# Prompt attention taken in pairs: one TensorE visit for two items, softmax statistics stored in runs, the samples' decoding queued at a group's last value slab

## The chip, the core and the metric

The kernel runs on one core of a Trainium2 chip. The metric is device time in microseconds (us), the median of three runs. The profile is of one further execution. TensorE is called PE in the rows (its weight loads PEld), VectorE is DVE, ScalarE is ACT, GpSimd is POOL, and SP is the queue from which nearly all DMAs are issued.

## What is computed

One layer of a decoder trunk for 1024 prompt tokens and 8 samples of 4 tokens, width 1024. Cut to what matters here:

```
h, B, C, q, k, v, g_conv, g_att = xn @ w_in          # q, k, v: 3 groups x 8 heads x 64
conv_out = (B * causal_conv3(C * h)) @ w_conv_out
for g, (window, dil) in enumerate(((128, 1), (512, 4), (2048, 16))):
    logits = q . k[t - i * dil] * scale + bias[i]    # i = 0 .. window / dil
    m = max(logits); p = exp(logits - m); s = sum(p); o_g = p @ v / s
o = merge of the three groups by their softmax denominators
x = x + gate1 * ((sig(g_conv) * conv_out + sig(g_att) * (o @ w_attn_out)) @ w_o)
x = x + gate2 * (relu(norm(x) @ w_mlp_in) ** 2 @ w_mlp_out)
```

The samples' tokens attend to caches of earlier keys and values (the decoding).

## The kernel before

All float32 products are made of three matmuls on split operands (high and low parts). The stages follow each other: gate and convolution projections, then q, k and v, then `w_conv_out`, `w_attn_out`, `w_o`, and the channel mixer.

**The stage of the change.** For each group in `ORDER` = (1, 2, 0) and each of its four pairs of heads (a *unit*), three slabs are projected: q, k and v. Each slab is three `gemm` calls of 24 matmuls (L375, 352 columns). `gemm` calls `slot()` after its 12th matmul and the main loop calls it again after the 24th, so a slot lies behind every 12 matmuls, 18 in a unit. After the last v chunk `add_unit` queues the unit's eight attention *items* (128 queries each, against one or two blocks of 128 keys, `nk`), and they are worked off inside the next unit's slots. After the last unit they run inside the stage of `w_conv_out`, which has 24 `gemm` calls and 48 slots.

**slot()** first runs what `later` holds as due, then lets the generator `attention` (in `bg`) advance while its credit lasts, then the two lanes of `paced` (the decoding and the merges), each of which says how many slots it rests. The credit grows by `rate` per slot: 0.85 of the queued `work` over 18 slots, 2200 after the last unit.

**One item** goes through three steps, pipelined over three items. `att_scores`: six matmuls of 64 rows (L974) into one `ps_s` and one `ps_g` bank, two adds of the bias with a maximum (L976, DVE), the negated maximum (L979), two exponentials (L982, ACT). `att_tr`: 2 x nk transposes by TensorE (L102) and a copy back. `att_pv`: 4 x nk matmuls of 64 columns (L1011) into `ps_o`. Between these steps the credit may run out, and then 12 projection matmuls come in between. Of the 96 items 44 have nk = 2.

**After a unit's last item** `att_pv` writes the maxima and sums (`st`) to `st_d` in DRAM, element by element: a unit's 128 x 32 numbers go as 4096 pieces of 4 bytes, in four DMAs (eight in group 2). `merge(j)` (L1222) reads them back and weights the three groups. PSUM banks: three of `ps_g` (the projections use them too), two of `ps_s`, one each of `ps_pt`, `ps_ss`, `ps_o`. `ps_ss` holds the sums of squares of q and k (L378, L379), read by a chain on ACT (L387 to L389) and DVE (L393).

**The decoding** `decode(g)` starts when the last item of the group's fourth unit is done; that of the last group runs after all attention, one step per slot. It uses `ps_s` and `ps_pt`.

Of the kernel before, what the change touches and what calls it, by code (L numbers as in the profile page):

```python
# [17 lines left out]
P = 128  # L18
# [21 lines left out]
NPG, NHF = 34, 5  # L40
# [9 lines left out]
class Trunk:  # L50
# [53 lines left out]
    def slot(self):  # L104
# [6 lines left out]
        while self.bg and self.credit > 0:  # L111
            try:
                cost = next(self.bg[0])
                if cost is None:
                    break
                self.credit -= cost
            except StopIteration:
                self.bg.popleft()
# [770 lines left out]
    def add_unit(self, g, j, q, k, v):  # L889
        u = dict(g=g, j=j, q=q, k=k, v=v, bias=self.bias, vt=None, O=None, st=None)  # L890
        tiles = self.attn_tiles(g)
        for i, tl in enumerate(tiles):
            self.items.append((u, tl, i == 0, i == len(tiles) - 1, i))
            self.work += 650 + 570 * tl[2]
        self.work += 600

    def values(self, u):
        nc, v = self.nc, u["v"]
        u["vt"] = vt = self.page("vt", (P, 8, P))
        for h in range(2):  # L900
            b = self.bank("s")
# [3 lines left out]
            del b  # L905
            yield None

    def sample_values(self, u):
        g, j = u["g"], u["j"]
        b = self.bank("pt")  # L910
        self.turn(b[0:32, 0:P], u["v"][:, NP:T], self.ident)
        self.evac(self.vnew[32 * g:32 * g + 32, j * P:(j + 1) * P], b[0:32, 0:P])

    def attention(self):
        st = {}
        s1 = s2 = last = None
        while True:
            it = self.items.popleft() if self.items else None
            if last is not None:
                self.sample_values(last)  # L920
                if last["g"] == ORDER[2]:
                    if last["j"] < 3:
                        self.paced[1].append(self.merge(last["j"]))
                elif last["j"] == 3:
                    self.paced[0].append(self.decode(last["g"]))
                last = None
                yield 100.0
            if it is None and s1 is None and s2 is None:
# [4 lines left out]
            if it is not None:  # L933
                if it[2]:
                    if it[0]["bias"] is None:
                        it[0]["bias"] = self.load_bias(it[0]["g"], it[0]["j"])
                    yield from self.values(it[0])
                self.att_scores(it, st)
                yield 650.0
            else:  # L940
                yield None
            if s1 is not None:
                self.att_tr(s1, st)
                yield 220.0 * s1[1][2]
            else:
                yield None
            if s2 is not None:
                self.att_pv(s2, st)
                yield 350.0 * s2[1][2]
                if s2[3]:  # L950
                    last = s2[0]
            s1, s2 = it, s1
        self.paced[1].append(self.merge(3))
        for g in (self.decode(ORDER[2]), self.sample_merge()):
            for n in g:
                for _ in range(n):
                    yield None

    def att_scores(self, it, st):
        nc = self.nc  # L960
        u, tl = it[0], it[1]
        q, k, bias = u["q"], u["k"], u["bias"]
        q0, k0, nk, b0, _, _ = tl
        N = nk * P
        ps = [self.bank(n) for n in "sg"]
        S = self.half("S")
        if u["st"] is None:
            u["st"] = self.sm.tile([P, 2, 2, 8], F32, name="st", tag="st", bufs=3)
        mx, sm = (u["st"][:, x, :, it[4]] for x in range(2))
        ng = self.sm.tile([P, 2], F32, name="ng", tag="ng", bufs=3)  # L970
        for x, (a, b) in enumerate((("hi", "hi"), ("hi", "lo"), ("lo", "hi"))):
            for hh in range(2):
                pr = slice(64 * hh, 64 * hh + 64)
                nc.tensor.matmul(ps[hh][:, :N], q[a][pr, q0:q0 + P], k[b][pr, k0:k0 + N], start=(x == 0), stop=(x == 2))  # L974
        for hh in range(2):
            nc.vector.tensor_tensor_reduce(  # L976
                out=S[:, hh * 256:hh * 256 + N], in0=ps[hh][:, :N], in1=bias[:, hh, b0:b0 + N],
                scale=1.0, scalar=LOW, op0=ALU.add, op1=ALU.max, accum_out=mx[:, hh:hh + 1])
        nc.vector.tensor_scalar(ng, mx, -1.0, None, op0=ALU.mult)  # L979
        for hh in range(2):  # L980
            s = S[:, hh * 256:hh * 256 + N]
            nc.scalar.activation(s, s, AF.Exp, bias=ng[:, hh:hh + 1], accum_out=sm[:, hh:hh + 1])  # L982
        st[id(it)] = S

    def att_tr(self, it, st):
        nk = it[1][2]
        S = st[id(it)]
        ps = self.bank("g" if it[4] % 2 else "pt")
# [7 lines left out]
    def att_pv(self, it, st):  # L996
# [27 lines left out]
        if last:  # L1024
# [3 lines left out]
            for x in range(2):  # L1028
                for hh in range(2):
                    row = sd[x, hh]  # L1030
                    if g == 0:
                        nc.sync.dma_start(out=row.rearrange("(t i) -> i t", i=P), in_=stt[:, x, hh])
                    elif g == 1:
                        nc.sync.dma_start(out=row.rearrange("(q i r) -> i r q", q=2, r=4),
                                          in_=stt[:, x, hh].rearrange("p (r q) -> p r q", q=2))
                    else:
                        for y in range(2):
                            nc.sync.dma_start(out=row.rearrange("(a t y) -> y a t", t=8, y=2)[y],
# [905 lines left out]
```

## Time and profile before

| | |
|---|---|
| time, median of 3 runs | 2187.48 us (2186.69 to 2188.03) |
| the profiled execution | 2182.63 us, of which the span is 2180.8 us |
| busy in the span | PE 2055.5 us (94%), DVE 1416.5 (65%), ACT 995.9 (46%), POOL 785.4 (36%) |
| mean granted clock of TensorE | 0.981 |

The span runs from the first to the last instruction. A share of the whole span is an average over stages. The rows further down are of the stages around the change.

### The profile page before, as it was taken

The page shows a single profiled execution, that of the slowest core. Times are in us where ns is not written, and L with a number is a line of the kernel's source. Part 1 is how long each engine was busy: PE and PEld are TensorE (multiplying, and loading weights), DVE is VectorE, ACT ScalarE, POOL GpSimd, SP SyncE. Part 2 cuts the span into 40 slices and gives each one's busy share as a digit, 9 for nine tenths or more (in the row PEclk, how much of TensorE's full clock was granted, in tenths as well). Part 3 has the DMA queues.
Part 4 walks back from the last instruction along what each step waited for, and adds up shares of the span by engine and source line. Part 5 has one row for each costly group of instructions (what it writes and reads, how often), then busy time and mean ns, then how long its engine had stood idle before and what let it go on. Part 6 is the DMA issues. An engine that isn't in the chain of part 4 may idle for free.

```text
span 2180.8 us, 38933 instructions
## 1 busy us (share of the span) xinstructions
PE 2055.5 (94%) x15092; PEld 1906.9 (87%) x15092; DVE 1416.5 (65%) x2973; ACT 995.9 (46%) x2195; POOL 785.4 (36%) x553
## 2 busy tenths in 40 slices
PE   5899999999999999999998799998999999999998
PEld 2799999889888888778877689998999998999998
DVE  4846666435555566566666488369444447999997
ACT  4522323335555655455545232346555557433332
POOL 3645565320111110100112113235333335788785
PEclk8999999999999999999998899999999999999999
DMA  7242221664144577766567894541337629556542
GB/s 282 74 131 64 75 73 41 231 215 148 46 59 53 58 150 138 147 122 113 125 166 105 183 313 152 186 137 68 141 148 290 249 85 338 208 186 215 204 152 106
DMA packets 180978, 325.85 MB, mean 149 GB/s; under 512 B 77113, under 2 KB 120761, under 8 KB 179769
## 3 DMA queue, kind: packets, MB, share of 16 engines
q1 hardware_dynamic: 180360, 323.17, 51.9%
q8 instruction: 118, 1.93, 0.5%
q14 instruction: 68, 0.55, 0.1%
q10 hardware_dynamic: 432, 0.20, 0.0%
HBM read 270.48 MB, written 112.07 MB: 175 GB/s over the span
## 4 chain that ended last, share of the span: by engine, by line
PE 52%; DVE 18%; DMA 5%; ACT 4%; issue 3%; SPq 1%; POOL 1%; another core or an unknown queue 0%; DVEq 0%; ACTq 0%; POOLq 0%
PE ps_g L375 23%; DVE acc L1707 5%; DVE wprod L160 4%; PE ps_g L262 3%; PE ps_s L262 3%; PE ps_s L263 3%; PE ps_g L264 3%; PE ps_s L264 3%; PE ps_g L263 3%; PE ps_o L1011 1%; DVE hl L1559 1%; PE ps_s L974 1%; DVE wlo L195 1%; DMA st_d<-st 1%; DMA sg<-gate_d 1%
## 5 line engine op out<-in xcount | busy, mean ns | idle before, releaser
L160 DVE TENSOR_TENSOR wprod<-wraw,wprod 128x512 fp32r<-128x512 f32 x276 | 269.9, 980 | 177.1 <-ACT wprod L156 176.9
L375 PE MATMUL ps_g<-xh,whi 128*128 128x352 f32 x1056 | 367.3, 348 | 12.5 <-ACT whi L191 5.1
L375 PE MATMUL ps_g<-xh,wlo 128*128 128x352 f32 x1056 | 346.3, 328 | 4.2 <-DVE wlo L195 4.1
L375 PE MATMUL ps_g<-xl,whi 128*128 128x352 f32 x1056 | 347.0, 329 | 3.0 <-POOL xl L404 2.1
L375 PEld LDWEIGHTS ps_g<-xh,whi 128*128 128x128 f32 x1056 | 203.1, 192 | 49.5 <-issue 25.5
L156 ACT CAST wprod<-wraw 128x512 fp32r<-128x512 f32 x276 | 163.3, 618 | 151.8 <-DVE wprod L160 104.6
L375 PEld LDWEIGHTS ps_g<-xl,whi 128*128 128x128 f32 x1056 | 203.1, 192 | 6.3 <-POOL xl L404 4.1
L375 PEld LDWEIGHTS ps_g<-xh,wlo 128*128 128x128 f32 x1056 | 202.7, 192 | 5.7 <-DVE wlo L195 5.7
L195 DVE TENSOR_TENSOR wlo<-wraw,whi 128x512 fp32r<-128x512 f32 x184 | 132.1, 760 | 47.6 <-PE ps_g L375 22.3
L160 POOL TENSOR_TENSOR lo<-qn,hi 128x1024 fp32r<-128x1024 f32 x12 | 34.0, 2833 | 358.0 <-ACT hi L156 332.9
L275 POOL TENSOR_TENSOR ps_z<-ps_z,ps_s 128x264 f32<-128x264 f32 x64 | 60.4, 946 | 252.7 <-DVE ps_s L274 252.0
L262 PE MATMUL ps_s<-th,wprod 128*128 128x264 f32 x512 | 145.7, 285 | 1.8 <-DVE ps_s L274 1.8
L262 PE MATMUL ps_g<-th,wprod 128*128 128x264 f32 x512 | 146.8, 287 | 0.0
L263 PE MATMUL ps_s<-tl,wprod 128*128 128x264 f32 x512 | 145.9, 285 | 0.0
L264 PE MATMUL ps_g<-th,wprod 128*128 128x264 f32 x512 | 145.8, 285 | 0.0
L263 PE MATMUL ps_g<-tl,wprod 128*128 128x264 f32 x512 | 145.5, 284 | 0.0
L264 PE MATMUL ps_s<-th,wprod 128*128 128x264 f32 x512 | 145.4, 284 | 0.0
L191 ACT CAST whi<-wraw 128x512 fp32r<-128x512 f32 x184 | 104.5, 619 | 54.8 <-DMA wraw<-in_w_conv_out 40.3
L982 ACT ACTIVATE S<-S,ng 128x128 f32<-128x128 f32 (+1 forms) x192 | 84.9, 443 | 93.1 <-DVE ng L979 91.4
L262 PE MATMUL ps_g<-xh,wprod 128*128 128x264 f32 x384 | 110.7, 288 | 4.6 <-ACT wprod L156 4.6
L262 PE MATMUL ps_s<-xh,wprod 128*128 128x264 f32 x384 | 110.5, 288 | 3.4 <-DVE ps_s L278 3.4
L264 PE MATMUL ps_g<-xh,wprod 128*128 128x264 f32 x384 | 110.3, 287 | 3.5 <-DVE wprod L160 3.5
(386 smaller groups left out, 6617.1 us busy)
## 6 DMA issues: line engine op xcount, KB each, us to landing
wraw<-in_w_in SPq DMA_DIRECT2D x76, 512.0 KB
wada<-in_w_ada SPq DMA_DIRECT2D x48, 512.0 KB
hid_d<-hid SPq DMA_DIRECT2D x32, 528.0 KB
wraw<-in_w_mlp_in SPq DMA_DIRECT2D x32, 512.0 KB
wraw<-in_w_mlp_out SPq DMA_DIRECT2D x32, 512.0 KB
hraw<-hid_d SPq DMA_DIRECT2D x56, 264.0 KB
kv<-in_v SPq DMA_DIRECT2D x28, 512.0 KB
wraw<-in_w_conv_out SPq DMA_DIRECT2D x24, 512.0 KB
```

What stands on the lines that cost most here:

```text
L156: nc.scalar.copy(hi, src)
L160: eng.tensor_tensor(out=lo, in0=src, in1=hi.bitcast(F32), op=ALU.subtract)
L191: self.nc.scalar.copy(hi[:, s], w[:, s])
L195: self.nc.vector.tensor_tensor(out=lo[:, s], in0=w[:, s], in1=hi[:, s].bitcast(F32), op=ALU.subtract)
L262: nc.tensor.matmul(ps, hi, xh, start=(k == 0), stop=False)
L263: nc.tensor.matmul(ps, hi, xl, start=False, stop=False)
L264: nc.tensor.matmul(ps, lo, xh, start=False, stop=(k == 3))
L275: nc.gpsimd.tensor_tensor(out=z[p], in0=z[p], in1=s[p], op=ALU.add)
L375: self.nc.tensor.matmul(ps, a, x, start=(i == 0), stop=(i == n - 1))
L974: nc.tensor.matmul(ps[hh][:, :N], q[a][pr, q0:q0 + P], k[b][pr, k0:k0 + N], start=(x == 0), stop=(x == 2))
L982: nc.scalar.activation(s, s, AF.Exp, bias=ng[:, hh:hh + 1], accum_out=sm[:, hh:hh + 1])
L1707: nc.vector.tensor_tensor(out=a, in0=a, in1=ps, op=ALU.add)
```

## The change

Items leave the queue two at a time. A *visit* is now one uninterrupted piece of work: the transposes of the pair before, the value products of the pair before that, then the scores of this pair, the two items side by side in two `ps_s` banks. A negative cost ends the slot's turn, so there is at most one visit in a slot. The value transposes move from `ps_s` to `ps_pt` and `ps_g`. `st` goes to DRAM in runs: of 128 bytes (group 0, after a VectorE transpose), 16 bytes (group 1) or 32 bytes (group 2); the merge reads group 2 into another place and reorders it with one copy. The samples' values are turned one slot after a unit's last v chunk, and the group's decoding is queued there too. The pools grow by one page and three half tiles, and the scratch for dynamic DMAs is set to 2048 bytes. Cut to its core:

```diff
--- before.py
+++ after.py
-NPG, NHF = 34, 5
+NPG, NHF = 35, 8
...
                 cost = next(self.bg[0])
                 if cost is None:
                     break
-                self.credit -= cost
+                self.credit -= abs(cost)
+                if cost < 0:
+                    break
...
-            self.work += 650 + 570 * tl[2]
-        self.work += 600
+            self.work += 450 + 450 * tl[2]
+        self.work += 4 * 400 + 1200
 
     def values(self, u):
...
-        for h in range(2):
-            b = self.bank("s")
+        for h, n in enumerate(("pt", "g")):
+            b = self.bank(n)
             for i in range(4):
                 self.turn(b[:, i * P:(i + 1) * P], v[:, (4 * h + i) * P:(4 * h + i + 1) * P], self.ident)
             self.evac(vt[:, 4 * h:4 * h + 4, :], b.rearrange("p (i f) -> p i f", i=4))
-            del b
-            yield None
-
-    def sample_values(self, u):
-        g, j = u["g"], u["j"]
+
+    def sample_values(self, g, j, v):
         b = self.bank("pt")
-        self.turn(b[0:32, 0:P], u["v"][:, NP:T], self.ident)
+        self.turn(b[0:32, 0:P], v[:, NP:T], self.ident)
         self.evac(self.vnew[32 * g:32 * g + 32, j * P:(j + 1) * P], b[0:32, 0:P])
+        if j == 3:
+            self.paced[0].append(self.decode(g))
+            if g == ORDER[2]:
+                self.paced[0].append(self.sample_merge())
 
     def attention(self):
         st = {}
...
+        p1 = p2 = None
         while True:
...
+            pair = [self.items.popleft() for _ in range(2)] if self.items else None
+            if pair is None and p1 is None and p2 is None:
                 if self.done:
                     break
                 yield None
                 continue
...
+            cost = 400
+            if pair is not None and pair[0][2]:
+                u = pair[0][0]
+                if u["bias"] is None:
+                    u["bias"] = self.load_bias(u["g"], u["j"])
+                self.values(u)
+                yield -1200
+            for it, n in zip(p1 or (), ("pt", "g")):
+                self.att_tr(it, st, n)
+                cost += 200 * it[1][2]
+            for it in p2 or ():
+                self.att_pv(it, st)
+                cost += 120 * it[1][2]
+            if pair is not None:
+                self.att_scores(pair, st)
+                cost += sum(450 + 130 * it[1][2] for it in pair)
+            yield -cost
+            if p2 is not None and p2[1][3] and p2[1][0]["g"] == ORDER[2]:
+                self.paced[1].append(self.merge(p2[1][0]["j"]))
+            p1, p2 = pair, p1
+
+    def att_scores(self, pair, st):
...
+        ps = [self.bank("s") for _ in range(2)]
...
+        if u["g"] == 1:
+            r = pair[0][1][4]
+            mx, sm = (u["st"][:, x, :, r:r + 5:4] for x in range(2))
+        else:
+            mx, sm = (u["st"][:, x, :, pair[0][4]:pair[0][4] + 2] for x in range(2))
+        ng = self.sm.tile([P, 2, 2], F32, name="ng", tag="ng", bufs=3)
+        for i, it in enumerate(pair):
...
+            for x, (a, b) in enumerate((("hi", "hi"), ("hi", "lo"), ("lo", "hi"))):
+                for hh in range(2):
+                    pr = slice(64 * hh, 64 * hh + 64)
+                    nc.tensor.matmul(ps[hh][:, 256 * i:256 * i + N], q[a][pr, q0:q0 + P], k[b][pr, k0:k0 + N],
+                                     start=(x == 0), stop=(x == 2))
+        for i, it in enumerate(pair):
+            N, b0 = it[1][2] * P, it[1][3]
+            S = st[id(it)] = self.half("S")
             for hh in range(2):
...
+                nc.vector.tensor_tensor_reduce(
+                    out=S[:, hh * 256:hh * 256 + N], in0=ps[hh][:, 256 * i:256 * i + N], in1=bias[:, hh, b0:b0 + N],
+                    scale=1.0, scalar=LOW, op0=ALU.add, op1=ALU.max, accum_out=mx[:, hh, i:i + 1])
         nc.vector.tensor_scalar(ng, mx, -1.0, None, op0=ALU.mult)
...
+        for i, it in enumerate(pair):
+            N, S = it[1][2] * P, st[id(it)]
+            for hh in range(2):
+                s = S[:, hh * 256:hh * 256 + N]
+                nc.scalar.activation(s, s, AF.Exp, bias=ng[:, hh, i:i + 1], accum_out=sm[:, hh, i:i + 1])
...
             sd = self.st_d[g][j]
-            for x in range(2):
-                for hh in range(2):
-                    row = sd[x, hh]
...
+            if g == 0:
+                tr = self.sm.tile([P, 32], F32, name="tr", tag="tr", bufs=2)
+                nc.vector.transpose(tr, stt.rearrange("p x h t -> p (x h t)"))
+                for b in range(4):
+                    nc.sync.dma_start(out=sd.rearrange("x h (t b i) -> b (x h t) i", b=4, i=32)[b], in_=tr[32 * b:32 * b + 32, :])
+            elif g == 1:
+                for x in range(2):
+                    for hh in range(2):
+                        nc.sync.dma_start(out=sd[x, hh].rearrange("(q i r) -> i q r", q=2, r=4),
+                                          in_=stt[:, x, hh].rearrange("p (q r) -> p q r", q=2))
+            else:
+                for y in range(2):
+                    nc.sync.dma_start(out=sd.rearrange("x h (a y t) -> y a (x h) t", y=2, t=8)[y],
+                                      in_=stt[64 * y:64 * y + 64].rearrange("p x h t -> p (x h) t"))
...
-            nc.sync.dma_start(out=wk[:, g], in_=self.st_d[g][j].rearrange("s h (b i) -> (h b) s i", i=16))
+            nc.sync.dma_start(out=M if g == 2 else wk[:, g], in_=self.st_d[g][j].rearrange("s h (b i) -> (h b) s i", i=16))
         yield 2
+        nc.vector.tensor_copy(wk[:, 2].rearrange("p s (t y) -> p s t y", y=2), M.rearrange("p s (y t) -> p s t y", y=2))
...
                     self.add_unit(g, j, st["q"], st["k"], st["v"]["v"])
+                    self.later.append((1, lambda g=g, j=j, v=st["v"]["v"]: self.sample_values(g, j, v)))
...
-    nc = _bacc.Bacc("TRN2", target_bir_lowering=False, num_devices=1)
+    nc = _bacc.Bacc("TRN2", target_bir_lowering=False, num_devices=1, dynamic_dma_scratch_size=2048)
```

## Rows read from the trace of the kernel before

**Rows 1.** Busy time by stretch (us; instructions), granted clock, DMA share, GB/s.
```profile
530.00:1175.00 645.00, 623.36 (x4420) 535.11 (x4420) 410.41 (x1118) 365.60 (x918) 80.42 (x38) 0.99 0.57 104
1175.00:1324.00 149.00, 125.09 (x897) 112.61 (x895) 94.42 (x227) 51.23 (x122) 19.90 (x14) 0.91 0.83 216
```

**Rows 2.** Timeline of PE around three visits: start us, us, engine, line, operation, count.
```profile
1004.58 0.32 PE L379 MATMUL ps_ss<-sql,blk_r 128*128 128x352 f32 x1
1004.83 0.44 PE L1011 MATMUL ps_o<-S,vt 128*64 128x128 f32 x4
...
1006.01 0.33 PE L375 MATMUL ps_g<-xl,whi 128*128 128x352 f32 x1
...
1141.91 0.32 PE L379 MATMUL ps_ss<-sql,blk_r 128*128 128x352 f32 x1
...
1142.39 0.28 PE L974 MATMUL ps_s<-lo,hi 64*128 64x256 f32 x1
...
1142.51 0.28 PE L974 MATMUL ps_s<-hi,lo 64*128 64x256 f32 x1
...
1142.98 0.32 PE L375 MATMUL ps_g<-xl,whi 128*128 128x352 f32 x1
...
1144.59 0.33 PE L375 MATMUL ps_g<-xh,wlo 128*128 128x352 f32 x1
1144.75 0.60 PE L102 MATMUL ps_pt<-ident,S 128*128 128x128 f32 x4
1145.28 0.66 PE L1011 MATMUL ps_o<-S,vt 128*64 128x128 f32 x8
...
1146.13 0.32 PE L375 MATMUL ps_g<-xl,whi 128*128 128x352 f32 x1
```

**Rows 3.** L974, all 96 items: what ended PEld's idle time before it (us, times).
```profile
  issue: 16.6, 78
```

**Rows 4.** Who PE waited for, 530 to 1175 us: total us, times, longest.
```profile
PE ps_ss L378 <- DVE sq L393: 5.7, 3, 3.1
PE ps_g L102 <- ACT S L982: 4.6, 2, 4.2
...
PE ps_pt L102 <- ACT S L982: 2.2, 3, 0.7
```

**Rows 5.** Who PE waited for, 1175 to 1324 us.
```profile
PE ps_pt L1064 <- DVE lm L1058: 10.0, 1, 10.0
PE ps_pt L1068 <- DVE dS L1065: 5.2, 1, 5.2
PE ps_g L974 <- DVE mc L1388: 5.0, 1, 5.0
```

**Rows 6.** The chain that ended last, in order of time: start us, us, what.
```profile
1167.06 20.24 DMA sg<-gate_d
...
1220.17 22.00 DMA st_d<-st
```

**Rows 7.** Three stretches with a low clock, columns as in rows 1, and their sum.
```profile
1236.00:1247.00 11.00, 3.27 (x12) 3.27 (x13) 1.35 (x3) 1.14 (x2) 0.00 (x0) 0.53 1.01 168
...
sum 29.00, PE 15.51 PEld 13.01 DVE 11.27 ACT 9.08 POOL 2.83; mean PE 5.17 PEld 4.33 DVE 3.76 ACT 3.03 POOL 0.94
```

**Rows 8.** A stretch after a wait of 4.2 us, columns as in rows 1.
```profile
1123.00:1128.00 5.00, 3.70 (x16) 3.50 (x17) 1.42 (x10) 2.81 (x10) 0.00 (x0) 0.66 0.85 299
```

**Rows 9.** Timelines of DVE, ACT and PE around one item's softmax.
```profile
1144.52 0.42 DVE L976 CUSTOM_DVE_ANT_0 S<-ps_s,bias 128x256 f32<-128x256 f32 x1
...
1145.32 0.17 DVE L979 TENSOR_SCALAR ng<-st 128x2 f32<-128x2 f32 x1
1145.40 0.53 DVE L393 SCALAR_TENSOR_TENSOR sq<-ps_ss,sq 128x352 f32<-128x352 f32 x1
...
1146.44 0.19 ACT L982 ACTIVATION_READ_ACCUMULATOR S<-S,ng 128x1 f32 x1
...
1147.90 0.32 PE L378 MATMUL ps_ss<-sqh,blk_r 128*128 128x352 f32 x1
```

More of the change, by code (lines that the diff above doesn't have):

```diff
@@ L932, in attention @@
                 continue
[L933 to L959, printed above, removed]
+            cost = 400
[5 more added lines that the diff above has]
+                yield -1200
@@ L960, in att_scores @@
+            p1, p2 = pair, p1
+    def att_scores(self, pair, st):
         nc = self.nc
-        u, tl = it[0], it[1]
+        u = pair[0][0]
         q, k, bias = u["q"], u["k"], u["bias"]
[L963 to L966, printed above, removed]
+        ps = [self.bank("s") for _ in range(2)]
         if u["st"] is None:
             u["st"] = self.sm.tile([P, 2, 2, 8], F32, name="st", tag="st", bufs=3)
-        mx, sm = (u["st"][:, x, :, it[4]] for x in range(2))
@@ L970, in att_scores @@
-        ng = self.sm.tile([P, 2], F32, name="ng", tag="ng", bufs=3)
-        for x, (a, b) in enumerate((("hi", "hi"), ("hi", "lo"), ("lo", "hi"))):
-            for hh in range(2):
-                pr = slice(64 * hh, 64 * hh + 64)
-                nc.tensor.matmul(ps[hh][:, :N], q[a][pr, q0:q0 + P], k[b][pr, k0:k0 + N], start=(x == 0), stop=(x == 2))
-        for hh in range(2):
-            nc.vector.tensor_tensor_reduce(
-                out=S[:, hh * 256:hh * 256 + N], in0=ps[hh][:, :N], in1=bias[:, hh, b0:b0 + N],
-                scale=1.0, scalar=LOW, op0=ALU.add, op1=ALU.max, accum_out=mx[:, hh:hh + 1])
@@ L979, in att_scores @@
-        nc.vector.tensor_scalar(ng, mx, -1.0, None, op0=ALU.mult)
[L980 to L985, printed above, removed]
+        if u["g"] == 1:
[3 more added lines that the diff above has]
+            mx, sm = (u["st"][:, x, :, pair[0][4]:pair[0][4] + 2] for x in range(2))
@@ new lines, in att_scores @@
+        ng = self.sm.tile([P, 2, 2], F32, name="ng", tag="ng", bufs=3)
+        for i, it in enumerate(pair):
+            q0, k0, nk, _, _, _ = it[1]
+            N = nk * P
+            for x, (a, b) in enumerate((("hi", "hi"), ("hi", "lo"), ("lo", "hi"))):
[3 more added lines that the diff above has]
+                                     start=(x == 0), stop=(x == 2))
@@ L986, in att_tr @@
+    def att_tr(self, it, st, bank):
         nk = it[1][2]
         S = st[id(it)]
-        ps = self.bank("g" if it[4] % 2 else "pt")
+        ps = self.bank(bank)
         for hh in range(2):
@@ L1027, in att_pv @@
             sd = self.st_d[g][j]
-            for x in range(2):
-                for hh in range(2):
-                    row = sd[x, hh]
[L1031 to L1038, printed above, removed]
-                                              in_=stt[64 * y:64 * y + 64, x, hh])
+            if g == 0:
[12 more added lines that the diff above has]
+                                      in_=stt[64 * y:64 * y + 64].rearrange("p x h t -> p (x h) t"))
     def decode(self, g):
```

14 lines of the change are left out of this document (1 added, 13 removed).

## The prediction

> **What bounds the kernel now.** I read the stretches first, then TensorE's timeline in the stage of the change, then who it waited for, then the chain that ended last. In the projection of q, k and v TensorE is busy in 623.4 of 645 us; in the stage that follows, where attention ends, in 125.1 of 149 us, and there the clock is lower (0.91) and the DMA share high (0.83) [rows 1]. DVE is busy in 410 and 94 us of the two, ACT less. So TensorE sets the end in both: what shortens its own work counts in full, and so does what ends its waits. The reader should see two different things: in the first stage little waiting and many short visits between the projection's products, in the second three long waits [rows 5].
>
> **What a visit costs.** The projection's products start 0.16 us apart (1144.59 to 1144.75) [rows 2]. From the last of them before a visit to the second after it would be 0.32 us without the visit; the rest is its price. A score visit: 1141.91 to 1142.98, so 1.07 - 0.32 = 0.75 us. Its six matmuls go in three couples 0.12 us apart (1142.39 to 1142.51), 0.36 us, so 0.39 us go for entering and leaving. A visit of four transposes and eight value products: 1144.59 to 1146.13, so 1.22 us. Four value products span 0.44 us and eight 0.66, so one costs 0.055; a lone one then spans 0.275 us, and if a transpose does too, four in 0.60 us are 0.108 apart. That leaves 1.22 - 0.43 - 0.44 = 0.35 us fixed, and as transposes follow the projection without a gap I put it on the value products' entry and exit. Where scores follow value products directly (1004.58 to 1006.01) the two cost 1.11 us against 0.57 + 0.75 apart: 0.21 saved [rows 2].
>
> **Term 1, fewer visits.** Before, each of 96 items has a score part and a value part; 78 of the score parts begin after a wait of PEld for nothing but the issue, 0.21 us each, which I read as a change of tile shape from the full array; the other 18 follow value products [rows 3]. Fixed costs: 96 x 0.39 + 96 x 0.35 - 18 x 0.21 = 67.2 us. After: 48 visits, in each the value products pass directly to the scores: 48 x (0.39 + 0.35 - 0.21) = 25.4 us. The products themselves stay. Saved: 41.8 us. The trace shows no twelve score matmuls in a row. If the second item's six paid the 0.39 us again, 18.7 us less would be saved, 23.1; I take the full sum, because within one item the second and third couple already run at 0.12 us.
>
> **Term 2, waits in the first stage that end.** TensorE waits 4.6 + 2.2 us for exponentials before transposes [rows 4]. A pair's visit costs 2200 to 3100 of credit and a slot earns 470 to 620 (0.85 of 10000 to 13150 over 18), so visits lie 4 to 5 slots apart, some 9 us; a pair's softmax (below) needs 3 to 6. These 6.8 us go; at worst they stay.
>
> **Term 3, new waits in the first stage.** (a) The pair takes both `ps_s` banks, and in the same slot the decoding, which runs after the visit, may want one. It has to wait for three of the pair's four maxima, each 0.4 us (1144.52 to 1145.32 for two) [rows 9]: 1.3 us with the way there. Groups 1 and 2 have 16 + 8 decoding steps with such a bank, and 4 of 18 slots hold scores: 5.3 x 1.3 = 7 us. Bounds 0 and 24 x 1.3 = 31. I take 7. (b) `ps_ss` is read by L393, which ended at 1145.93, and the next sums started at 1147.90: 2.0 us of slack [rows 9]. A pair puts two more maxima (0.8 us) and, where ACT's chain lies behind it, two more exponentials with their sums (1145.49 to 1146.63, 1.1 us) ahead of it, which just uses the slack up. The wait there is 5.7 us now [rows 4]. I add 4 us; bounds 0 and 1 us for each of 48 visits. Queued behind such a wait is the whole projection.
>
> **Term 4, the three long waits of the second stage.** 10.0, 5.2 and 5.0 us [rows 5]. The third is `mc`, which waits for the gate's chunk `sg`, 20.24 us under way; on the chain `st_d` itself takes 22.00 us [rows 6]. Both times the queue holds 4096 elements of 4 bytes: 5.4 ns for each. As runs, group 0 has 128, group 2 512, group 1 1024; at the same price for one they take 0.7, 2.7 and 5.5 us. The decoding's constants, for which `lm` waited 10.0 us, are now requested about one slot after the last v chunk, before the last unit's statistics are there to be stored. So 20.2 us go. During and after these waits TensorE ran 15.5 us of products in stretches at a granted 0.51 to 0.53, which is the lower of its levels, 1.2 instead of 2.4 GHz [rows 7]: half of that, some 7 us, goes too. Sum 27 us; nothing of it goes if the transfers stay as slow. SP gains as well: six DMAs fewer per unit of group 2.
>
> The Trainium skill, "DMA: Bandwidth & Descriptors", Specifications, says that a transfer under 512 bytes falls short of line rate because it turns into a read-modify-write. The new runs of 16 to 128 bytes are all below that. If by this rule a piece costs the same whatever its length, the counts above hold and the sum stays; if the queue stays clogged by read-modify-writes, term 4 is lost and the sum is 2158. The trace, where 16 KB took 22 us, agrees that small pieces are slow; it shows no run of 16 or 128 bytes of this kind.
>
> **Term 5, new waits in the second stage.** Here a slot earns 2200, so the credit lets a visit into nearly every slot until the 4 pairs, the values and the two last passes are through (18800 in all, 8 to 9 slots). Three visits in a row then find only 12 products, 1.93 us, between a pair's scores and its transposes. The pair's softmax: four maxima 1.6 us, negation 0.2, four exponentials 2.2: 4.0 us, the first item's two ready after 2.9. In the row the first maximum also started 1.7 us after the last score matmul (1142.79), behind other DVE work [rows 9]. So the first transposes wait 1.0 to 2.7 us and the second item's 0.6 more; I take 2.5 us. A wait of 4.2 us was followed by a clock of 0.66 over 5 us, where 3.7 us of products lost a third, 1.3 us [rows 8]; I charge it each time. 3 x (2.5 + 1.3) + 0.9 for the visit after = 12 us. Bounds 0 and 6 x 5 = 30.
>
> **Term 6.** The second stage moves 216 GB/s over 149 us, 32 MB [rows 1]; in about 130 us it needs 247 GB/s. I add 3 us for loads that come late; bounds 0 and 15.
>
> **At nothing.** Statistics' transposes and the merge's copy (4 and 4 small DVE instructions; DVE idles a third of the time), 48 negations fewer, the larger pools, value transposes in other banks, the scratch (DMAs go from SP and ACT). Without DVE's slack the first two cost under 4 us.
>
> **Sum.** -41.8 - 6.8 + 7 + 4 - 27 + 12 + 3 = -49.6 us. The profiled execution took 2182.63 us, so 2133.0. The median of the runs lies 4.85 us above it: 2138 us.
>
> **Rivals.** *Cheaper still*: terms 3, 5 and 6 don't appear, as DVE and ACT keep up. 2138 - 26 = 2112. For it: DVE is busy in 64% of the stage. Against: the slack of 2.0 us is thin. Chance 0.19. *The second item pays for its own scores*: 2138 + 19 = 2157. Chance 0.12. *The DMA queue stays clogged* (the long waits stay, less 7 us because the decoding asks earlier): 2138 + 20 = 2158. Against it is the count of pieces. Chance 0.12. *Slower*: pairs make bursts on ACT and DVE, and the projection stops at `ps_ss` at every one of 72 sums of squares. The terms without 3 give 61 us, so it decides from 61 / 72 = 0.85 us per sum on; at 1.2 us each 2213 us with term 3a left out, for the slack to be gone everywhere. Against: only 5.7 us of such waits now, and three quarters of the slots hold no pair's scores. Chance 0.04. *No change*: shorter visits only move TensorE's idle time elsewhere, if DVE's order of work sets the pace. Against: TensorE is busy in 97% of the stage. Chance 0.03.
>
> **Numbers.** The forecast (2124 to 2155) has 0.50. The range from 2106 to 2171 leaves out the slower case, no change, and the tails of the others. A measurement of this kernel tells about 0.2% (4.4 us) from no change. Faster by more: 0.50 + 0.19 + 0.12 + 0.12 = 0.93; within: 0.03; slower: 0.04.
>
> **What the profile after would show.** Term 1: 48 groups of twelve L974 products in both `ps_s` banks, PEld's idle time for the issue before L974 down from 16.6 to about 9 us or less. Term 2: waits of L102 for exponentials gone before 1140 us and (term 5) some 8 us of them after it. Term 3: the decoding's products waiting for `st`, L378 for L393, a few us each. Term 4: `st_d` landing in under 6 us, no wait of `lm` or `mc` over 3 us. I am wrong if the stretch of q, k and v shrinks by less than 20 us, or if waits of a new kind sum to more than 40 us.

## The result and the profile after

The changed kernel took 2169.94 us (2166.61 to 2171.84, 4 runs) against 2187.76 us (2186.69 to 2189.42) beside it: 17.8 us less, ratio 0.9916, 95% interval 0.9899 to 0.9933. The forecast had the sign; it counted on 49.6 us, and the range's upper end, 2171, only just holds the time. The profiled execution took 2169.99 us, with a span of 2168.2 us.

The stretches of the changed kernel, columns as in [rows 1]: the projection of q, k and v, the stage of `w_conv_out` (the second stage), and the stage of `w_attn_out`.

```profile
530.00:1159.00 629.00, 585.86 (x4381) 529.28 (x4380) 403.17 (x1076) 359.09 (x911) 76.99 (x37) 0.99 0.33 105
1159.00:1305.00 146.00, 128.64 (x936) 116.26 (x936) 100.19 (x237) 51.39 (x129) 20.22 (x13) 0.94 0.72 226
1305.00:1357.00 52.00, 48.51 (x290) 47.98 (x290) 37.06 (x61) 16.91 (x36) 25.12 (x24) 0.97 0.51 166
```

The first stretch is 16 us shorter than before; less than 20 was the prediction's own sign of being wrong. TensorE's busy time fell by 37.5 us (623.4 to 585.9), but length less busy time, its idle time, rose from 21.6 to 43.1 us. The second is 3 us shorter, and TensorE's busy time there rose by 3.6 us. The third was 46.3 us before.

One visit at the full clock, TensorE's timeline:

```profile
748.93 0.32 PE L377 MATMUL ps_g<-xh,wlo 128*128 128x352 f32 x1
749.09 0.38 PE L102 MATMUL ps_pt<-ident,S 128*128 128x128 f32 x2
749.31 0.60 PE L102 MATMUL ps_g<-ident,S 128*128 128x128 f32 x4
749.84 0.88 PE L1009 MATMUL ps_o<-S,vt 128*64 128x128 f32 x12
750.64 0.33 PE L967 MATMUL ps_s<-hi 64*128 64x128 f32 x2
...
750.92 0.27 PE L967 MATMUL ps_s<-hi,lo 64*128 64x128 f32 x2
751.03 0.33 PE L967 MATMUL ps_s<-hi 64*128 64x256 f32 x2
...
751.32 0.28 PE L967 MATMUL ps_s<-hi,lo 64*128 64x256 f32 x2
...
751.79 0.32 PE L377 MATMUL ps_g<-xl,whi 128*128 128x352 f32 x1
```

From 748.93 to 751.79 less 0.32 it costs 2.54 us. By the forecast's prices, 6 transposes (0.65), 12 value products (0.66), twelve score products in six couples at 0.12 us (0.72) and 0.53 fixed make 2.56. The couples start 0.11 to 0.17 us apart, and the second item's first one (751.03) only 0.11 us behind the first item's last. PEld's idle time for the issue before the scores (L967, all 48 pairs) fell from 16.6 us [rows 3] to this:

```profile
  issue: 8.3, 47
```

Who TensorE waited for, in the first stage and then in the second and third (total us, times, longest), to set beside [rows 4, 5]:

```profile
PE ps_ss L380 <- DVE sq L395: 18.9, 10, 4.3
PE ps_pt L102 <- ACT v L96: 6.8, 6, 2.3
PE ps_pt L102 <- DVE v L99: 4.7, 5, 1.6
PE ps_s L1124 <- DVE st L973: 2.7, 1, 2.7
PE ps_s L1137 <- DVE st L973: 2.3, 3, 0.8
...
PE ps_pt L102 <- DVE v L99: 4.3, 1, 4.3
PE ps_pt L102 <- DVE so L1204: 3.9, 2, 3.6
PE ps_s L1137 <- DMA kv<-in_k1T: 3.8, 3, 1.8
PE ps_pt L102 <- DVE dS L1065: 3.5, 1, 3.5
PE ps_pt L102 <- ACT S L981: 2.4, 2, 2.2
PE ps_g L377 <- ACT oh L158: 2.3, 1, 2.3
...
```

The waits for exponentials in the first stage and the three long waits of the second are gone, but for 3.5 us for `dS` ahead of other transposes. In their place stand `ps_ss` (5.7 us before), a wait that no term of the forecast had, that of the samples' turn (`L102` for `v`: 11.5 us and 4.3 at the border), and in the second and third stage many of one to four us.

The statistics' storing, `st_d`, from issue to landing in the three groups in the order 1, 2, 0; a landing is recorded for about half of them, and the last of the three rows holds the merges' reads as well:

```profile
DMA to landing us min/median/max: 4.2/5.6/6.0
...
DMA to landing us min/median/max: 2.0/4.2/4.9
...
DMA to landing us min/median/max: 1.4/1.4/3.3
```

Before, one of a unit's four, 1024 pieces of 4 bytes in a queue of 4096, took 22.00 us [rows 6].

**One wait for `ps_ss`.** Timelines of TensorE, ACT and DVE:

```profile
1132.38 0.43 PE L380 MATMUL ps_ss<-sqh,blk_r 128*128 128x352 f32 x1 [4.32 <-DVE sq L395]
...
1124.68 0.49 ACT L981 ACTIVATE S<-S,ng 128x256 f32<-128x256 f32 x1
...
1126.96 0.50 ACT L391 ACTIVATE sq<-r 128x352 f32<-128x352 f32 x1
...
1129.37 2.53 DVE L162 TENSOR_TENSOR ol<-og,oh 128x1024 fp32r<-128x1024 f32 x1 [2.73 <-ACT oh L158]
1131.82 0.51 DVE L395 SCALAR_TENSOR_TENSOR sq<-ps_ss,sq 128x352 f32<-128x352 f32 x1
```

ACT ends the chain that L395 needs at 1127.46, after the pair's exponentials. But L395 stands in DVE's order behind a merge's split `ol`, which waits 2.73 us for ACT and takes 2.53: 4.4 us pass before it starts. Of the nine longer waits three end behind decoding or a merge on DVE, one (1.27 us, at 1123.63) behind the pair's four maxima, the other five behind splits or a chain that themselves waited for ACT or took long. But one step further back the pair's softmax does stand: in six of the nine its four exponentials lie on ACT directly ahead of the square or the cast for which DVE then stood idle for 1.9 to 2.5 us. So before the wait of 2.63 us at 1004.82:

```profile
999.53 0.49 ACT L981 ACTIVATE S<-S,ng 128x256 f32<-128x256 f32 x1
...
1000.49 0.34 DVE L160 CAST sqh<-sq 128x352 fp32r<-128x352 f32 x1 [2.50 <-ACT sq L694]
...
1004.24 0.53 DVE L395 SCALAR_TENSOR_TENSOR sq<-ps_ss,sq 128x352 f32<-128x352 f32 x1
```

Between the last two rows lie a split, the weights' splits and eight copies of the decoding.

### The profile page after: what moved, and what is told of

The parts are those of the page before. It is cut to its first block, busy times and chain, and to the rows that moved or that the text cites. A ratio compares the mean times of both kernels' runs of the same rounds, so it can differ in the third digit from the quotient of the medians.

```text
span 2168.2 us, 38902 instructions
## 1 busy us (share of the span) xinstructions
PE 2023.1 (93%) x15092; PEld 1907.6 (88%) x15092; DVE 1414.0 (65%) x2933; ACT 991.2 (46%) x2195; POOL 783.5 (36%) x553
## 4 chain that ended last, share of the span: by engine, by line
PE 59%; DVE 20%; ACT 5%; issue 3%; DMA 2%; POOL 2%; SPq 0%; DVEq 0%; POOLq 0%; ACTq 0%
PE ps_g L377 23%; PE ps_g L264 4%; PE ps_s L264 4%; PE ps_s L265 4%; PE ps_g L266 4%; PE ps_s L266 4%; PE ps_g L265 4%; DVE acc L1709 4%; DVE wprod L162 4%; ACT S L981 1%; PE ps_s L967 1%; PE ps_o L1009 1%; DVE S L973 1%; DVE wlo L197 1%; DVE hl L1561 1%
## 5 line engine op out<-in xcount | busy, mean ns | idle before, releaser
L377 PE MATMUL ps_g<-xh,whi 128*128 128x352 f32 x1056 | 355.5, 337 | 12.7 <-ACT whi L193 6.4
L264 PE MATMUL ps_s<-th,wprod 128*128 128x264 f32 x512 | 146.2, 286 | 1.7 <-DVE ps_s L276 1.7
L264 PE MATMUL ps_g<-th,wprod 128*128 128x264 f32 x512 | 146.7, 287 | 0.0
L265 PE MATMUL ps_s<-tl,wprod 128*128 128x264 f32 x512 | 145.9, 285 | 0.0
```

The source lines that it names most:

```text
L264: nc.tensor.matmul(ps, hi, xh, start=(k == 0), stop=False)
L265: nc.tensor.matmul(ps, hi, xl, start=False, stop=False)
L377: self.nc.tensor.matmul(ps, a, x, start=(i == 0), stop=(i == n - 1))
```

## The experiments

The table holds all runs. Stages run from the first product of `xh` in the q projection to that of `ybh`, of `oh` and of `mh` in TensorE's timeline; idle is TensorE's, the sum of its gaps there. Kernels of one group ran on one chip, with the kernel before beside them: 2179.89 us (2170.88 to 2185.81) in A, 2199.29 in B, 2181.77 in C, 2197.93 in D, 2180.53 in E. What lies ahead of the stages, the same in all, took 509 to 517 us, so the stages tell more than the time.

| run | group | time us | ratio (95%) | q, k, v / idle | second / idle | third |
|---|---|---|---|---|---|---|
| before | | 2187.76 | 1 | 661.8 / 21.6 | 148.4 / 23.9 | 46.3 |
| after | | 2169.94 | 0.9916 (0.9899 to 0.9933) | 645.5 / 43.3 | 145.5 / 17.2 | 51.9 |
| a_turn2 | A | 2153.18 | 0.9892 (0.9856 to 0.9927) | 634.4 / 30.1 | 145.1 / 17.9 | 49.6 |
| a_ssgate | A | 2181.75 | 1.0014 (0.9997 to 1.0032) | 654.7 / 49.0 | 145.9 / 18.2 | 58.7 |
| a_no_dec | A | 2195.01 | 1.0078 (1.0048 to 1.0109) | 681.7 / 54.2 | 146.7 / 17.8 | 48.8 |
| b_runs | A | 2153.27 | 0.9887 (0.9856 to 0.9918) | 654.6 / 17.2 | 130.2 / 9.3 | 46.3 |
| bc | B | 2173.25 | 0.9882 (0.9867 to 0.9898) | 660.7 / 21.0 | 141.4 / 15.8 | 46.4 |
| ab | B | 2161.18 | 0.9823 (0.9804 to 0.9842) | 643.4 / 34.8 | 140.7 / 14.5 | 50.2 |
| a_sscopy | B | 2157.91 | 0.9816 (0.9792 to 0.9839) | 634.2 / 32.7 | 149.1 / 20.0 | 49.3 |
| a_rate | B | 2152.32 | 0.9784 (0.9767 to 0.9802) | 637.2 / 30.6 | 143.2 / 15.5 | 46.2 |
| after2 | C | 2170.66 | 0.9938 (0.9918 to 0.9959) | 645.6 / 42.0 | 144.6 / 15.9 | 49.2 |
| b_runs2 | C | 2152.61 | 0.9862 (0.9836 to 0.9889) | 653.2 / 16.9 | 130.2 / 9.3 | 46.3 |
| a_rate_late | C | 2162.03 | 0.9898 (0.9878 to 0.9918) | 637.2 / 31.0 | 153.9 / 22.4 | 46.4 |
| ab_rate | C | 2157.93 | 0.9884 (0.9861 to 0.9906) | 635.8 / 31.3 | 150.2 / 18.6 | 46.4 |
| a_order | D | 2153.45 | 0.9793 (0.9763 to 0.9822) | 641.3 / 30.2 | 140.5 / 11.6 | 46.3 |
| a_tail | D | 2147.87 | 0.9769 (0.9743 to 0.9796) | 639.5 / 30.6 | 137.3 / 13.1 | 46.2 |
| a_rate_pre | D | 2154.48 | 0.9800 (0.9768 to 0.9831) | 637.2 / 29.4 | 146.2 / 16.4 | 46.3 |
| b_pre | D | 2163.06 | 0.9835 (0.9806 to 0.9864) | 655.0 / 16.2 | 132.9 / 10.5 | 46.2 |
| a_tail2 | E | 2146.34 | 0.9844 (0.9830 to 0.9857) | 637.0 / 30.5 | 139.9 / 13.6 | 46.2 |
| b_runs3 | E | 2156.11 | 0.9890 (0.9872 to 0.9907) | 652.1 / 17.3 | 130.1 / 9.4 | 46.3 |

**The samples' turn one slot later (a_turn2).** An entry of 1 in `later` falls due in the very next `slot()`, right behind the copy of the last v chunk out of its bank.

```diff
-self.later.append((1, lambda ...: self.sample_values(g, j, v)))
+self.later.append((2, lambda ...: self.sample_values(g, j, v)))
```

> The changed kernel, with the turn of the samples' values two slot calls after it is queued instead of one. Theory: one call means the same slot in which the last v chunk's copy has just been issued, so TensorE stands 0.8 to 4.3 us before it, 14 us more in the twelve units than before; one slot later the copy is done and these waits of the v turn fall under 3 us in sum: 2157 us (13 less than the changed kernel). Rival: the copy is late because DVE and ACT are behind, and the next transposes or ps_ss wait in its place: 2166 to 2170 us, with the waits of L380 up by as much.

The first stage fell by 11.1 us and its idle time by 13.2. The waits for `v` fell from 15.8 to 0.9 us there, while those for `st` rose from 6.7 to 11.5; the first rows now:

```profile
PE ps_ss L380 <- DVE sq L395: 15.2, 8, 4.3
PE ps_s L1173 <- DVE st L973: 5.7, 4, 2.0
```

The theory holds: one slot, with 12 projection products in it, covers the copy.

**No visit while `ps_ss` is open (a_ssgate).** The loop over the attention's pieces also asks that no sum of squares waits for its reader.

```diff
-while self.bg and self.credit > 0:
+while self.bg and self.credit > 0 and not self.ss_open:
```

> The changed kernel, but no visit in a slot in which a sum of squares has just been put into ps_ss (the visit waits until its reader L395 is issued, one slot later). Theory: L395 is late because a pair's maxima and copies, issued between the sum and L395, stand ahead of it on DVE and ACT; then the waits of L380 fall from 18.7 us to under 6 us and the time to about 2158 us. Rival: L395 is late from ACT's load in general (squares, weights' casts, exponentials), and the waits stay above 13 us: 2168 us or more, as later visits put more work into the second stage.

Idle time rose by 5.7 us; `ps_ss` still cost 14.8 us, the turn's waits grew to 15.8 us in that stage, and the third stage took 58.7 us. By the numbers the rival holds, L395 late from ACT's load in general. The run does not clear the pair's own softmax, though, because the gate left it in the way: a visit now begins with `ps_ss` free, but the next sum follows one slot later, while that softmax still runs. In 11 of the 12 waits the pair's exponentials again lie directly ahead of the square for which DVE stood 1.1 to 2.5 us. The longest wait (lines moved by one to three here):

```profile
1015.48 0.49 ACT L984 ACTIVATE S<-S,ng 128x256 f32<-128x256 f32 x1
...
1016.44 0.34 DVE L161 CAST sqh<-sq 128x352 fp32r<-128x352 f32 x1 [2.49 <-ACT sq L695]
...
1020.75 0.43 PE L381 MATMUL ps_ss<-sqh,blk_r 128*128 128x352 f32 x1 [3.79 <-DVE sq L396]
```

No run took the exponentials out of ACT's way, so their share is read from the traces and not shown by an experiment.

**`ps_ss` copied away by ACT (a_sscopy).** On top of a_turn2, L395 reads a chunk in its place.

```diff
+sc = self.chunk("ssc"); nc.scalar.copy(sc, ss)
-self.later.append((1, lambda: scale(ss, r0)))
+self.later.append((1, lambda: scale(sc, r0)))
```

> The changed kernel with the later turn (2153.2 us), and the sums of squares copied out of ps_ss by ACT right behind its chain, so that L395 on DVE reads the copy and ps_ss is free without DVE. Theory: in slots without a visit the projection comes back to ps_ss after 3.9 us, before DVE, in its order, has read it; with the copy the 15.2 us of waits of L380 fall under 5 us and the time to about 2143 us. Rival: ACT is as late as DVE, since the pair's exponentials stand ahead of its chain; the waits stay above 10 us and 72 more copies of 0.45 us delay ACT further: 2153 us or more.

```profile
PE ps_s L1175 <- DVE st L975: 6.7, 4, 2.3
PE ps_ss L380 <- ACT ssc L704: 5.5, 4, 2.3
...
PE ps_g L102 <- ACT v L96: 2.6, 1, 2.6
```

The wait shrank from 15.2 to 5.5 us, the idle time not at all (32.7 against 30.1): the wait moved to the next buffer that DVE or ACT empties late. Freeing `ps_ss` alone gained nothing; the 72 copies are also new work for ACT, and the run does not tell what they cost.

**The runs alone (b_runs, b_runs2, b_runs3).** The kernel before with the new storing in `att_pv`, the merge's copy and the scratch (not separated from each other); items single, decoding as before.

```diff
-nc.sync.dma_start(out=row.rearrange("(t i) -> i t", i=P), in_=stt[:, x, hh])
...
+nc.vector.transpose(tr, stt.rearrange("p x h t -> p (x h t)"))
...
+nc.sync.dma_start(out=sd.rearrange(...)[b], in_=tr[32 * b:32 * b + 32, :])
```

> The kernel before, with only the second part of the change: statistics stored in runs (and the small scratch that makes room for it). Theory: the three waits of 10.0, 5.2 and 5.0 us come from the 4096 elements per unit; they go and the low clock behind them: 22 to 27 us less, about 2162 us, st_d lands within 6 us. Rival: the order of loads in SP's queue makes them, whatever the statistics cost: 2180 us or more, waits of lm and dS still over 8 us in sum.

> Single items, statistics in runs, again beside the others. Both theories: near 2153 us, second stage 130 us. If the changed kernel were the better one on an equal chip, it would lie below this; I expect it 15 to 20 us above.

26.6 us gained in A, 29.2 in C, 24.4 in E: more than the whole change. Who TensorE waited for in the second stage of b_runs:

```profile
PE ps_s L1140 <- DMA kv<-in_k1T: 5.2, 3, 2.9
PE ps_g L375 <- DVE wlo L195: 1.5, 1, 1.5
...
```

The waits of [rows 5] are gone, and the granted clock from 1166 to 1296 us is 0.97 against 0.91. So the changed kernel loses 15 us in the second stage against its own part. after2, beside b_runs2 on one chip, repeats this: 144.6 against 130.2.

> The changed kernel again, beside the other three of this group, since the kernel before, with its many 4-byte pieces, took 2179.9 to 2199.3 us from chip to chip. Both theories: near 2168 to 2172 us, second stage 145 us, 16 us of waits ahead of the samples' turn.

**Which part gives that back? bc, ab, a_no_dec.** bc is b_runs with the decoding queued early and the turn in the second slot behind the last v chunk, as in a_turn2, items single; ab is the changed kernel with the decoding behind the last item again and the turn in a `ps_g` buffer.

```diff
 # bc, in sample_values of b_runs
+if j == 3:
+    self.paced[0].append(self.decode(g))
...
 # bc, behind the last v chunk
+self.later.append((2, lambda ...: self.sample_values(g, j, v)))
...
 # ab, behind a pair's last value product
+self.later.append((1, lambda u=u: self.sample_values(u["g"], u["j"], u["v"])))
+elif u["j"] == 3: self.paced[0].append(self.decode(u["g"]))
```

> The kernel before with the second and third parts of the change (runs; the samples' turn two slot calls after the last v chunk and the decoding queued there), items still one by one. With the second part alone it took 26.6 us less than before. Theory: the third part by itself is worth little, as the last group's decoding waited for nothing but its own loads: 2 to 5 us less than the second part alone, and the second stage stays near 130 us. Rival: it is the third part that makes the second stage long (decoding and attention share ps_pt, ps_s and DVE): 10 us or more above the second part alone, with the stage at 140 us or more.

> The changed kernel without its third part: decoding queued after a group's last value products, the samples' turn one slot after them and through ps_g, so that it doesn't stand ahead of the next transposes in ps_pt. Theory: pairs save their 38 us of TensorE work in the first stage and lose some 12 to ps_ss; with the second stage at 130 us as in the second part alone, about 2140 us. Rival: it is the pairs that make the second stage long: then the stage stays near 145 us and the time is about 2155 us.

> The changed kernel without its third part: the samples' values are turned and the decoding is queued after the last value products of a unit, as before, and that of the last group after all attention (but in the paced lane). Theory: the waits of the v turn (14 us) go, as the turn comes long after the copy; the second stage gets longer by some 5 us because the last group's decoding starts some 10 slots later and ends in the flush: about 2160 us. Rival (the earlier decoding is what pays for the second stage): the wait of lm for its constants comes back with 5 to 10 us and the time is 2170 to 2180 us.

Either part alone lengthens the second stage, by 11.2 us (bc) and 10.5 (ab) over b_runs, and both together by 15; the theories of bc and ab, a stage near 130 us, fell. The two ran on another chip than b_runs, but kernels that ran on several chips differ in this stage by at most 2.6 us (b_runs 130.1 to 130.2, a_tail 137.3 and 139.9). a_no_dec missed both its ranges and is no clean undo: it puts the turn's transpose into `ps_pt` directly ahead of the next visit, whose transposes then wait for its copy:

```profile
PE ps_pt L102 <- DVE vnew L99: 17.1, 7, 3.8
```

TensorE's granted clock was at its lower level for 71.7 us of that stage (6.8 in the changed kernel). So it says little of the decoding itself.

**Faster pacing (a_rate), then the last decoding behind the visits again (a_rate_late, ab_rate).**

```diff
 # a_rate, on a_turn2
-self.rate = self.work / 18 * 0.85
+self.rate = self.work / 18
...
 # a_rate_late, in sample_values
-if j == 3:
+if j == 3 and g != ORDER[2]:
...
 # a_rate_late, at the end of attention()
+self.paced[0] += [self.decode(ORDER[2]), self.sample_merge()]
```

ab_rate is ab with the factor 1.0.

> The changed kernel with the later turn (2153.2 us), and the credit at 1.0 instead of 0.85 of the queued work per unit, so that less attention is left for the second stage. Theory: the second stage is 145 us long because more value products and transposes are left for it than before (92 and 38 against 60 and 30) and visits there come in a row; it shrinks by 8 us or more, the first grows by 3: about 2148 us. Rival: what is left over is the last unit itself, which the rate doesn't move, and the stage is long for its loads and DVE's order: 2153 us, stage above 142 us.

> Pairs, turn one slot later, visits paced at the whole rate; only the last group's decoding is queued behind the last visit again. Theory (that decoding, begun some slots earlier, meets the four items that pairs leave for the second stage, in its PSUM buffer and in VectorE's queue): the second stage falls from 143 to 134-138 us with the other stages as they were, 2143 to 2147 us in all. Rival (the decoding costs its time wherever it lies, and behind the visits it comes out late for the samples' merge): the second stage stays at 141 to 146, 2149 to 2156 us.

> Pairs and runs alone: the samples' turn one slot behind the unit's last value product, in a buffer of ps_g, every group's decoding behind it, visits at the whole rate. Theory (earlier decoding is what lengthens the second stage): 134 to 138 us there and 640 to 643 in the first, 2146 to 2151 us in all. Rival (the pairs alone lengthen it): 140 to 143 us there, 2153 to 2158 us.

With the whole rate the third stage is back at 46.2 us, without waits for `oh` and `ol`; the second fell by 1.9 us (145.1 in a_turn2), where the theory wanted 8. My theory of the early decoding fell: put behind the visits, the second stage took 153.9 us in place of 143.2, and 150.2 in ab_rate. With single items the early decoding costs (bc), with pairs at the whole rate the late one does; at the factor 0.85 it did not (ab 140.7, a_turn2 145.1). Why the sign turns stays open.

**Spreading the last visits (a_tail), loading the merges' parts earlier (a_rate_pre, b_pre).** All but b_pre on a_rate.

```diff
 # a_tail
-self.rate = 2200.0
+self.rate = 1200.0
...
 # a_rate_pre and b_pre, in merge(): group g + 1 is loaded before the rest for g
+nxt = loads(g + 1) if g < 2 else None
-yield 3
+yield 2 if g else 5
```

> The same kernel with the visits left for the second stage paced at 1200 a slot instead of 2200, about one pair visit in two slots. Theory (a pair visit in each of four slots in a row is what leaves TensorE waiting and at the low clock there): idle in the second stage falls from 15.5 to below 11 us and its low clock from 12 to below 8, the stage from 143 to 136-139, unless the last merge comes late (a few us in the attention's output stage). Rival (the waits belong to merges and decoding, wherever the visits lie): 141 to 148 us, and 2 to 6 us more in the stage behind it.

> The pairs, turn one slot later, whole rate; the merges load the next group's part one step ahead (same number of slots). Theory (VectorE stands in its queue for merges' loads, 11 us in the second stage, and what it owes TensorE is late by that): VectorE's waits for them there fall below 4 us, TensorE's idle from 15.5 to 8-12, 2142 to 2147 us. Rival (those waits are covered, or the earlier pages push others): no less than 2149 us.

> Single items, statistics in runs, and the same earlier loads in the merges. Theory: VectorE's waits for them in the second stage fall from 10.5 to below 4 us and TensorE's idle there from 9.3 to 5-8: 2148 to 2151 us. Rival: 2151 to 2155 us.

a_tail brought the second stage to 137.3 us and the kernel to 2147.87, within what the theory gave for the stage; but idle (13.1 us, 15.5 in a_rate) and time at the lower clock (13.6 us, 12.2 in a_rate) stayed above its bounds, so the burst is only a part. Earlier loads cut VectorE's waits for them from 11.0 us in a_rate to 1.3, and the stage grew to 146.2; these waits then stood at the head of its list:

```profile
DVE wlo L197 <- ACT whi L193: 18.5, 7, 4.3
```

For a_rate_pre the rival holds: the waits for loads were covered. b_pre took 2163.06 us, above both its ranges, on another chip than b_runs; its second stage took 132.9 us with 10.5 idle, where b_runs had 130.2 with 9.3, so the theory fell there too.

**The order within a visit (a_order).** Value products ahead of the transposes, on a_rate.

> Pairs, turn one slot later, whole rate, and within a visit the value products go ahead of the transposes, so that the transposes (whole-array) stand between the value products and the scores (half-array both): each of the 48 pair visits has two excursions into half-array forms where it had one. Theory (the fixed price belongs to a change of form, 0.35 to 0.39 us for each excursion, 0.21 less where two half-array forms meet directly): TensorE's time without idle in the first stage rises from 606.6 us by 44 x 0.2 to 44 x 0.4, to 615-624 us. Rival (the price belongs to the visit as such): it stays at 605 to 609 us.

The same visit in a_rate and then in a_order, from the last sum of squares to the first scores:

```profile
1007.13 0.32 PE L381 MATMUL ps_ss<-sql,blk_r 128*128 128x352 f32 x1
1007.29 0.60 PE L102 MATMUL ps_pt<-ident,S 128*128 128x128 f32 x4
1007.73 0.60 PE L102 MATMUL ps_g<-ident,S 128*128 128x128 f32 x4
1008.26 1.09 PE L1009 MATMUL ps_o<-S,vt 128*64 128x128 f32 x16
1009.28 0.39 PE L967 MATMUL ps_s<-hi 64*128 64x256 f32 x2
```

```profile
1007.33 0.32 PE L381 MATMUL ps_ss<-sql,blk_r 128*128 128x352 f32 x1
1007.59 1.09 PE L1009 MATMUL ps_o<-S,vt 128*64 128x128 f32 x16
1008.61 0.66 PE L102 MATMUL ps_pt<-ident,S 128*128 128x128 f32 x4
1009.11 0.60 PE L102 MATMUL ps_g<-ident,S 128*128 128x128 f32 x4
1009.63 0.39 PE L967 MATMUL ps_s<-hi 64*128 64x256 f32 x2
```

2.15 against 2.30 us: the second excursion costs 0.15 us. Without idle time the first stage rose from 606.6 to 611.1 us, below the theory's 615 and above the rival's 609. Only 26 excursions were added there, as not every visit holds all three parts; 26 x 0.15 = 3.9 of the 4.5 us. A change of form has its price, but a smaller one than expected.

**Pairs against single items on one chip (a_tail2, b_runs3).**

> Pairs with the turn one slot later, the whole rate and the second stage at 1200 a slot, beside single items with the runs on one chip. Theory (the pairs' smaller cost in the first stage outlasts what they add in the second once the visits there are spread): 2146 to 2150 us, 3 to 7 us below the other. Rival (the difference was that between two chips): within 2 us of the other.

> Single items, statistics in runs, beside the spread pairs on one chip. Both theories: 2151 to 2155 us.

2146.34 us (2144.22 to 2146.89) against 2156.11 (2153.52 to 2160.25). Of the 9.8 us, 4.7 lie ahead of the stages (509.1 and 513.8 us), where the kernels do the same; the first stage gives 15.1 and the second takes back 9.8. So some 5 us are the pairs' own, within the 3 to 7 that the theory gave. Second stage of a_tail2 and of b_runs3:

```profile
1146.00:1286.00 140.00, 126.40 (x928) 115.75 (x927) 102.88 (x240) 52.03 (x126) 25.75 (x16) 0.93 0.70 221
```

```profile
1166.00:1296.00 130.00, 120.56 (x892) 107.93 (x890) 96.53 (x230) 51.08 (x122) 23.26 (x14) 0.97 0.78 247
```

Pairs leave 36 more TensorE instructions to this stage. Busy time is 5.8 us more, and that is about what the clock takes: TensorE was busy for 17.0 us at the lower level against 4.3, where the projection's products start 0.29 us apart instead of 0.16. Idle time is 4.2 us more. So a_tail is the best version run: faster than the kernel before and the changed one.

## Why the prediction was right and wrong

The steps that failed: term 3b (4 us of waits at `ps_ss` counted, 13.2 measured), the samples' turn, which was given no wait and cost 15.8, and term 5 with the drain that it left out (the second and third stage were to shrink by 15.5 us and grew by 2.7).

**Term 1 was right in kind and over-sized.** 44 of the 48 visits lie in the first stage: 41.8 x 44 / 48 = 38.3 us expected, 37.5 less busy time measured. That it agrees so well is in part luck. 32 value products and 11 transposes moved on to the second stage, some 3 us at the forecast's prices, and TensorE was busy for 6.8 us at the lower clock in the first stage where it had been 13.1, some 3 us more. Over both stages time without idle fell by 34.3 us (764.7 to 730.4), and by about 31 without the clock's part (21.2 us of it at the lower clock, 27.7 before), of 41.8. A part of the difference is the price of a score visit, taken from one that cost 0.75 us; 37 lone ones at the full clock cost 0.71 on average. The rival of the second item's scores is out: its first couple follows at 0.11 us.

**Term 2 was right**, 6.8 us gone. **Term 3a** was over-sized: 6.7 us of waits for `st` in the first stage, 4.6 more than the decoding had waited there before, 7 more expected. The row before:

```profile
PE ps_s L1137 <- DVE st L976: 2.1, 2, 1.5
```

**Term 3b was mis-sized**: 4 us added, 13.2 measured (5.7 to 18.9). The mechanism was right, the pair's exponentials ahead of ACT's chain and the slack of 2.0 us used up. But I priced it as 1.1 us of ACT and 0.8 of DVE that "just uses the slack up". The rows show a longer path: DVE, too, stands 1.9 to 2.5 us for ACT's square or cast behind the four exponentials (1.5 to 1.6 behind two, in the three waits before), and what lies in its order after that (splits, the decoding, a merge) comes on top before L395.

**A term was missing, the samples' turn.** The prediction took it, with the decoding's constants, as a step "about one slot after the last v chunk" and gave it no wait. It stands right behind that chunk's copy, 12 times: 15.8 us of waits (1.3 for the copies of `v` before). a_turn2 shows it. This and term 3b make up the error of the first stage: its idle time was to rise by 4 us and rose by 21.5.

**Term 4 was right as a mechanism**: b_runs shows the transfers short, the long waits gone and 24 to 29 us gained, where 27 were counted. The size was met by luck: the 27 were all to come from the second stage, which gave 18.2, and 7.2 came from the first, where none were counted. The rule of the Trainium skill ("DMA: Bandwidth & Descriptors", Specifications: transfers below 512 bytes fall short of line rate) did not keep the queue clogged: runs of 16 to 128 bytes landed in 1.4 to 6.0 us where pieces of 4 bytes, 4096 in the queue, took 22.0. That rival is out. A price by the count of pieces fits; but their number and their length changed together, and no run separates the two.

**Term 5 named the wrong waits.** Those for exponentials in the second stage were 2.6 us, not 8. (Its 18800 of credit is 16160 by the costs in the code, 7 to 8 slots.) In their place came a sum that I had not worked out: pairs hold four items in the pipeline where single items hold two, so more products, copies and softmax fall behind the last projection, together with the decoding and merges there. The 15.5 us are 27 and the 3.5 left of term 1, less 12 and 3; the 2.7 are 194.7 to 197.4. That pairs and early decoding each do it is shown by ab and bc; that the burst of visits is a part by a_tail, 3 to 6 us. The remaining 7 to 10 us against single items are idle time and a lower clock in about equal parts. Through which of the many small waits they come stays open: deferring the decoding at the whole rate and loading earlier made the stage longer, not shorter.

**Term 6** did not show as a late load: the moved bytes rose to 226 GB/s, and the waits for `kv` are 3.8 us, 2.0 before; 3 us more were counted.

## What to carry to other kernels

When an edit shortens the engine that sets the end, ask not only what that engine saves but which buffers the others must now empty sooner; a step put "one slot later" must be followed through the queue's own counting. Small DMA pieces are counted first: replacing a unit's 4096 of them was worth more than the whole rework around it. A deeper pipeline leaves more work behind the end of the stage that hides it (43 TensorE instructions here), so the drain is priced as a stage of its own, and paced. And the engine that a wait names is only its last step: ask what that engine stood for before.

## What the runs showed that was not expected

A wait of one in-order engine moves rather than goes: with `ps_ss` freed by a copy its wait fell by 9.7 us and TensorE's idle time rose by 2.6, ACT having 72 copies more to do. An excursion into half-array products costs 0.15 us more where whole-array transposes are put in its middle, not the 0.2 to 0.4 us that a_order expected from isolated excursions. The kernel before took 2180 to 2199 us in five groups of runs on five chips.
